# Seventy chunks of U products ahead of the V products in the first layer, where sixty-four were

## The chip, the cores and the metric

The kernel runs on one core of a Trainium2 chip. The metric is the time of one execution on the device in microseconds (us): the median of three runs of the kernel before is 2871.74 us (2870.99 to 2872.57). TensorE is called PE here, its weight loads PEld, VectorE DVE, ScalarE ACT, GpSimd POOL and SyncE SP.

## The reference

Two layers work on 256 latent tokens and 256 context tokens of width 1024. The first layer mixes tokens with a gated MLP, the second with a bidirectional state-space scan (S5); after each mixer comes a PEER block, in which every token picks experts out of 16384. The PEER block is what the change is about:

```python
def block(hb):
    q = (hb @ w_q).reshape(PEER_BLOCK, PEER_HEADS, 2, PEER_DHALF)
    s = jnp.einsum("nhkd,hkmd->nhkm", q, sub_keys)
    s_half, i_half = lax.top_k(s, PEER_TOPK)
    cand = s_half[:, :, 0, :, None] + s_half[:, :, 1, None, :]
    top_s, top_c = lax.top_k(cand.reshape(...), PEER_TOPK)
    ...
    ids = k1 * PEER_KEYS + k2
    g = jax.nn.softmax(top_s, axis=-1)
    ue = jnp.take(u_tab, ids, axis=0)
    ve = jnp.take(v_tab, ids, axis=0)
    act = jax.nn.gelu(jnp.einsum("nd,nhkd->nhk", hb, ue))
    return jnp.einsum("nhk,nhkd->nd", g * act, ve)
```

Each token so uses 8 heads x 16 experts = 128 rows of the table U (16384 x 1024) and the same 128 rows of the table V.

## The kernel before

**Two ways through the PEER block.** In the first layer (layer 0 in the code) 384 of the 512 tokens go through all 16384 experts densely, with a gate matrix that is zero where a token did not pick an expert. The tables are cut into 128 chunks of 128 experts. The other 128 tokens, the last of the context, go by gathers: POOL issues an indirect DMA (line 600) that brings one 4 KB row of U or V for each of 128 tokens, 512 KB in all; for a row of U DVE makes dot products (`gscr`, line 610), for a row of V it adds to the sum `acc` (line 623). There are 128 gathers of U and 128 of V, in turns of 16, into four buffers (`ROWS`); an issue waits until DVE has used the buffer four rows earlier.

**U product of a chunk** (`front`): the loads `ur` (512 KB), its split into a high part `uh` on ACT and a rest `ul` on DVE, 24 matmuls over 384 columns (lines 304 to 306; three for each of eight blocks, since the product of split numbers needs three), and a gelu on ACT (`act`, line 717). **V product of a chunk** (`back`): the load `vr` (512 KB), its split into `vh` (ACT) and `vl` (DVE), the gated activations `w` and their split `wh`, `wl`, and 18 matmuls over 512 columns (lines 753 to 755) that add into six PSUM banks. It also brings 192 KB of gates (`Gr`), and 192 KB of activations (`actr`) where the U product was made long before and its `act` written to memory (`act_d`).

**Order.** `dense` runs three stretches. First come the U products of the first `ahead` = `AHEAD0` chunks; between them stands the routing (top 16, one-hot products) and the building of the gates of three blocks of 128 tokens on DVE, PE and ACT (lines 641 to 679). All but the last two of these U products come before the end of the gate work. Of the activations all but the last `keep` = 8 are written to memory. Then the V products alone, until chunk `ahead - keep`; beside them run the phase tables of the second layer (lines 905 to 932), a few modulation rows (`adasv`, line 218) and the first 18 steps (36 rows) of the gathers. From there on one U and one V product alternate, and after the last U product eight V products follow. The gathers' other 110 steps are spread over this stretch.

```python
for k1 in range(ahead - TF[i]):
    front(k1, k1 < ahead - keep)
    during(k1)
between()
with tc.issue_after(ends["gates"]):
    for k1 in range(ahead - TF[i], ahead):
        front(k1)
...
for k1 in range(KEYS):
    if ahead <= k1 + keep < KEYS:
        front(k1 + keep)
        done += 1
    back(k1)
    done += 1
    pump(done / total)
```

In that last loop PE's order is the written one. On the other engines, and on PE ahead of it, a scheduler sets the order when the kernel is built, from due times of its own; each engine then runs its list strictly in turn. At the end `add_back` transposes the four sums on PE (line 586) and DVE adds them to the token state `XT` (line 328). The second layer starts with the norm of all 512 tokens and so needs the gathered sum `acc` too; its loads `kT` and `wqT` stand on SP behind the last use of the gathers' buffers, its first weights `s5w`, split into `s5wh` (ACT) and `s5wl` (half on DVE, half on POOL), behind the transposes of the dense sums.

Of the kernel before, what the change touches and what calls it, by code (L numbers as in the profile page):

```python
# [42 lines left out]
NST = 64  # L43
L = 8
NDENSE = 384
AHEAD0 = 64
TAIL0 = 0
WB = 2
KEEP0 = 8
# [57 lines left out]
def tile_hybrid(ctx: ExitStack, tc: tile.TileContext, I, out, stop=None):  # L107
# [15 lines left out]
    def use_banks(*b):  # L123
        banks[0] = list(b)
# [6 lines left out]
    def pool(name, bufs=1, side=None):  # L131
        return tc.tile_pool(name=name, bufs=bufs, side=side, reuse_waits="tile")
# [72 lines left out]
    def ada_rows(pa, blocks, cB=None, e=nc.vector):  # L205

        k = "g" if e is nc.gpsimd else "v"
        if cB is None:
            cB = ada_silu(pa)
        for i, f in blocks:  # L210
            w = pa.tile([P, D], F32, name=f"adat{k}")
            r0 = f * P - (0 if i else 3 * D)
            load(w, I[f"ada_t{i}"][r0:r0 + P, :])
            nt = parts_of(i, f)
            for t in range(nt):
                if e is nc.vector:
                    scr = pa.tile([P, D], F16, name=f"adas{k}", bufs=1)
                    e.scalar_tensor_tensor(scr, w, 1.0, cB[:, t], op0=OP.mult, op1=OP.mult,  # L218
                                           accum_out=mod[:, i, f, t:t + 1])
                else:  # L220
                    scr = pa.tile([P, D], F32, name="adap", bufs=1) if t == 0 else w
                    e.tensor_tensor(scr, w, cB[:, t], op=OP.mult)
                    nc.scalar.activation(scr, scr, AF.Copy, accum_out=mod[:, i, f, t:t + 1])
            if f % 8 == 7:
                m = mod[:, i, f - 7:f + 1, 0:nt]
                nc.vector.tensor_tensor(m, m, ab[:, i, f - 7:f + 1].unsqueeze(2).to_broadcast([P, 8, nt]), op=OP.add)
                scale_cols(i, f - 7, 8)
            yield
# [1009 lines left out]
    def spread(*items):  # L1238

        state = [[g, n, a, b, 0] for g, n, a, b in items]  # L1240

        def pump(t):
            for s in state:
                g, n, a, b, _ = s
                while s[4] < n * min((t - a) / (b - a), 1.0):
                    s[4] += next(g, None) or 1
        return pump

    def layer0():
# [53 lines left out]
        with pool("hx") as ph, pool("hold", side="right") as pk, ExitStack() as hold:  # L1303
# [57 lines left out]
            with pool("de0", 2) as pd, ExitStack() as rs:  # L1361
# [4 lines left out]
                def during(k):  # L1366
                    first((k + 1) / (AHEAD0 - TAIL0 - TF[0]))

                def between():
# [5 lines left out]
                    ada = ada_rows(pa, LATE[NS:NQ], cB)  # L1375
                    cut = (AHEAD0 - KEEP0) / (2 * KEYS - AHEAD0)
                    rest.append(spread((gathers, MID0, 0.0, cut), (gathers, 128 - early - MID0, cut, GEND), (phases, 29, *PW),
# [4 lines left out]
                def back_work(t):  # L1382
                    with tc.issue_after(ends["w"]) if PB_ <= t < PC_ else ExitStack():
                        rest[0](t)

                use_banks(2, 3, 4, 5, 6, 7)
                dense(pd, lambda: rs.enter_context(pool("db0", 2, side="right")), 0, n, hh, hl, AHEAD0, KEEP0, (0, 1), (2, 3, 4, 5, 6, 7),
                      during, between, back_work)
# [173 lines left out]
```

## Time and profile before

| | |
|---|---|
| median of three runs | 2871.74 us |
| the profiled execution: its own time | 2873.85 us |
| its span, first to last instruction | 2872.1 us |
| PE busy | 2640.3 us, 92% |
| DVE busy | 2233.4 us, 78% |
| mean granted clock of TensorE | 0.955 |

The dense part of the first layer lies from 492 us (gelu of its first U product) to 1735 us (last gathered row added) of the span. Rows of "windows" give for a stretch the busy time of each engine with the number of instructions, the granted clock and the DMA engines' mean busy share. A row of a timeline is one instruction, or several of one kind merged: start, duration, engine, line, operation, what it writes and reads, and in brackets how long the engine sat idle before it and what ended that.

### The profile page before, as it was taken

What the parts mean: (1) busy time and instruction counts of PE and PEld (TensorE: products, weight loads), DVE (VectorE), ACT (ScalarE), POOL (GpSimd) and SP (SyncE); (2) the same over time, 40 slices, a digit from 0 to 9 for tenths busy, and PEclk for the clock granted to TensorE, in tenths of its full rate; (3) what the DMA queues carried; (4) which work ended last, traced back from release to release, by engine and by line L of the source; (5) the groups of instructions that cost most, each with busy time, mean ns of one, the idle gap of its engine ahead of it and who ended that gap; (6) DMA issues with size and microseconds to landing.
All of it is one profiled execution on the core that took longest, in us unless ns stands there. A gap on an engine that the chain in (4) does not pass through costs nothing.

```text
span 2872.1 us, 43897 instructions
## 1 busy us (share of the span) xinstructions
PE 2640.3 (92%) x16231; PEld 2360.2 (82%) x16231; DVE 2233.4 (78%) x3964; ACT 1233.6 (43%) x1900; POOL 562.6 (20%) x429
## 2 busy tenths in 40 slices
PE   6799979998968899999999987898899999999998
PEld 2499878998956677999999976898888988899997
DVE  7795889999978677888888876474899867755555
ACT  5453242364653233333333324334456654444443
POOL 2032121000100212544444441235300000000000
PEclk8899989999979999999999998999899999999999
DMA  8569843564758888999999988996468989866652
GB/s 274 169 214 352 276 157 130 177 214 169 251 212 288 305 295 275 355 339 338 339 338 338 333 300 297 329 328 176 142 208 276 316 287 296 264 205 214 212 200 103
DMA packets 414560, 738.76 MB, mean 257 GB/s; under 512 B 41605, under 2 KB 272261, under 8 KB 409225
## 3 DMA queue, kind: packets, MB, share of 16 engines
q1 hardware_dynamic: 310240, 507.84, 53.2%
q0 software_dynamic: 36864, 134.23, 13.1%
q10 hardware_dynamic: 67240, 93.88, 9.3%
q8 instruction: 127, 2.08, 0.3%
q14 instruction: 89, 0.72, 0.1%
HBM read 633.07 MB, written 102.77 MB: 256 GB/s over the span
## 4 chain that ended last, share of the span: by engine, by line
PE 51%; DMA 8%; DVE 7%; issue 3%; ACT 1%; POOL 1%; SPq 0%; ACTq 0%; DVEq 0%; POOLq 0%
PE bk L754 8%; PE bk L306 8%; PE bk L755 8%; PE bk L304 8%; PE bk L753 8%; PE bk L305 8%; DMA vr<-peer_v 2%; PE bk L553 1%; DMA row<-peer_v,ids 1%; DVE vl L298 1%; DMA ph_d<-ph 1%; DVE ul L298 1%; DMA actr<-act_d 1%; DMA wp<-wpo 1%; PE bk L1151 1%
## 5 line engine op out<-in xcount | busy, mean ns | idle before, releaser
L304 PE MATMUL bk<-hxh,uh 128*128 128x384 f32 (+1 forms) x2048 | 644.4, 315 | 23.1 <-ACT act L717 14.4
L306 PE MATMUL bk<-hxh,ul 128*128 128x384 f32 (+1 forms) x2048 | 641.1, 314 | 14.0 <-DVE ul L298 14.0
L305 PE MATMUL bk<-hxl,uh 128*128 128x384 f32 (+1 forms) x2048 | 638.8, 312 | 0.0
L754 PE MATMUL bk<-vl,wh 128*128 128x512 f32 x1280 | 510.4, 399 | 26.0 <-DVE vl L298 24.5
L753 PE MATMUL bk<-vh,wh 128*128 128x512 f32 x1280 | 506.8, 396 | 24.1 <-ACT vh L296 16.9
L755 PE MATMUL bk<-vh,wl 128*128 128x512 f32 x1280 | 506.7, 396 | 0.6 <-DVE wl L298 0.6
L296 ACT ACTIVATE uh<-ur 128x1024 fp32r<-128x1024 f32 x256 | 271.5, 1061 | 512.4 <-PE bk L305 446.2
L304 PEld LDWEIGHTS bk<-hxh,uh 128*128 128x128 f32 x2048 | 394.2, 192 | 33.3 <-ACT act L717 19.1
L298 DVE TENSOR_TENSOR ul<-ur,uh 128x1024 fp32r<-128x1024 f32 x256 | 313.0, 1223 | 136.0 <-ACT uh L296 134.6
L306 PEld LDWEIGHTS bk<-hxh,ul 128*128 128x128 f32 x2048 | 393.5, 192 | 18.3 <-DVE ul L298 18.3
L305 PEld LDWEIGHTS bk<-hxl,uh 128*128 128x128 f32 x2048 | 394.2, 193 | 4.6
L298 DVE TENSOR_TENSOR vl<-vr,vh 128x1024 fp32r<-128x1024 f32 x256 | 313.1, 1223 | 50.0 <-ACT vh L296 40.8
L296 ACT ACTIVATE wh<-w 128x384 fp32r<-128x384 f32 (+1 forms) x256 | 120.6, 471 | 494.2 <-PE bk L754 465.1
L754 PEld LDWEIGHTS bk<-vl,wh 128*128 128x128 f32 x1280 | 244.6, 191 | 83.3 <-DVE vl L298 34.1
L753 PEld LDWEIGHTS bk<-vh,wh 128*128 128x128 f32 x1280 | 244.9, 191 | 77.5 <-ACT vh L296 20.8
L296 ACT ACTIVATE vh<-vr 128x1024 fp32r<-128x1024 f32 x256 | 268.0, 1048 | 82.9 <-DMA vr<-peer_v 69.2
L755 PEld LDWEIGHTS bk<-vh,wl 128*128 128x128 f32 x1280 | 244.5, 191 | 52.7 <-DVE wl L298 1.6
L298 DVE TENSOR_TENSOR wl<-w,wh 128x384 fp32r<-128x384 f32 (+1 forms) x256 | 125.6, 491 | 165.3 <-ACT wh L296 158.1
L600 POOL DMA_INDIRECT row<-peer_u,ids x128 | 169.3, 1323 | 274.7 <-DVE gscr L610 166.7
L600 POOL DMA_INDIRECT row<-peer_v,ids x128 | 163.8, 1280 | 239.0 <-DVE acc L623 162.2
L218 DVE SCALAR_TENSOR_TENSOR adasv<-adatv,cB 128x1024 f16<-128x1024 f32 x112 | 148.8, 1329 | 55.8 <-DMA adatv<-ada_t 54.7
L623 DVE SCALAR_TENSOR_TENSOR acc<-row,wts,acc 128x1024 f32<-128x1024 f32 x127 | 162.6, 1281 | 13.3 <-DMA row<-peer_v,ids 12.7
(324 smaller groups left out, 4453.0 us busy)
## 6 DMA issues: line engine op xcount, KB each, us to landing
ur<-peer_ut SPq DMA_DIRECT2D x256, 512.0 KB
vr<-peer_v SPq DMA_DIRECT2D x256, 512.0 KB
gd<-Gs ACTq DMA_DIRECT2D x40, 1024.0 KB
adatv<-ada_t SPq DMA_DIRECT2D x72, 512.0 KB
wqT<-peer_w_q SPq DMA_DIRECT2D x64, 512.0 KB
Gr<-gd SPq DMA_DIRECT2D x120, 192.0 KB
wp<-wpo ACTq DMA_DIRECT2D x32, 512.0 KB
wpi<-wp SPq DMA_DIRECT2D x16, 1024.0 KB
```

The costliest lines, as they stand in the source:

```text
L218: e.scalar_tensor_tensor(scr, w, 1.0, cB[:, t], op0=OP.mult, op1=OP.mult, accum_out=mod[:, i, f, t:t + 1])
L296: nc.scalar.activation(hi, src, AF.Copy)
L298: return e.tensor_tensor(lo, src, hi.bitcast(F32), op=OP.subtract)
L304: nc.tensor.matmul(o, ah, bh, start=(i == 0), stop=False)
L305: nc.tensor.matmul(o, ah, bl, start=False, stop=False)
L306: last = nc.tensor.matmul(o, al, bh, start=False, stop=(i == n - 1))
L553: nc.tensor.matmul(pm[:, d * P:(d + 1) * P], ws[b][:, ds], kT[:, b], start=(b == 0), stop=(b == 1))
L600: tc.keep_in_program_order(nc.gpsimd.indirect_dma_start(out=r[:], out_offset=None, in_=I[f"peer_{table}{i}"], in_offset=bass.IndirectOffse ...
L623: nc.vector.scalar_tensor_tensor(acc, r, w, acc, op0=OP.mult, op1=OP.add)
L753: nc.tensor.matmul(o, wh[:, js], vh[:, qs], start=first, stop=False)
L754: nc.tensor.matmul(o, wh[:, js], vl[:, qs], start=False, stop=False)
L755: nc.tensor.matmul(o, wl[:, js], vh[:, qs], start=False, stop=last)
```

## The change

One number: `AHEAD0` goes from 64 to 70.

```diff
-AHEAD0 = 64
+AHEAD0 = 70
```

Seventy U products then stand in the first stretch, 68 of them between the gate work; 62 of their activations are written to memory and read back, where 56 were. 62 V products stand alone before the alternation begins, where 56 did, and 58 pairs follow, where 64 did. The count of products, of gates and of gathered rows stays. The steps of the gathers are counted out over the new numbers: 36 rows over the V products alone, the others up to 97% of the alternation.

On DVE, at the end of the first stretch, where the gates of the third block are built (`eq` and `o` are one-hot matrices, `ul` is the split for a U product). Before:

```order
L675 TENSOR_TENSOR eq<-iot,kt_7736 128x2048 x3
L647 CAST gt_7738<-gs 128x128
L648 TENSOR_TENSOR gt_7738<-gs,gt_7738 128x128
L679 TENSOR_TENSOR o_7745<-eq,gt_7738 128x1024
L679 TENSOR_TENSOR o_7784<-eq,gt_7738 128x1024
L679 TENSOR_TENSOR o_7810<-eq,gt_7738 128x1024
```

At the same place of DVE's list now:

```order
L298 TENSOR_TENSOR ul<-ur,uh 128x1024 x2
L675 TENSOR_TENSOR eq<-iot,kt_7906 128x2048 x3
L647 CAST gt_7908<-gs 128x128
L298 TENSOR_TENSOR ul<-ur,uh 128x1024
L648 TENSOR_TENSOR gt_7908<-gs,gt_7908 128x128
L679 TENSOR_TENSOR o_7949<-eq,gt_7908 128x1024
```

Before, no split of a U product stood in the third block until its end; now five stand among its first rows (three of them here, two a few rows on), and the gates of the second block have 21 U products beside them where 18 were.

On DVE, from the split of the last V product on (`acc` is one gathered row, `XT` a sum added to the token state). Before:

```order
L298 TENSOR_TENSOR vl<-vr,vh 128x1024
L623 SCALAR_TENSOR_TENSOR acc<-row,wts,acc 128x1024 x5
L328 SCALAR_TENSOR_TENSOR XT<-bk_15830,mod,XT 128x128 x4
L328 SCALAR_TENSOR_TENSOR XT<-bk_15839,mod,XT 128x128 x4
L623 SCALAR_TENSOR_TENSOR acc<-row,wts,acc 128x1024
L328 SCALAR_TENSOR_TENSOR XT<-bk_15851,mod,XT 128x128 x4
L328 SCALAR_TENSOR_TENSOR XT<-bk_15860,mod,XT 128x128 x4
L623 SCALAR_TENSOR_TENSOR acc<-row,wts,acc 128x1024
L328 SCALAR_TENSOR_TENSOR XT<-bk_15872,mod,XT 128x128 x4
L328 SCALAR_TENSOR_TENSOR XT<-bk_15881,mod,XT 128x128 x4
L328 SCALAR_TENSOR_TENSOR XT<-bk_15891,mod,XT 128x128 x4
L328 SCALAR_TENSOR_TENSOR XT<-bk_15900,mod,XT 128x128 x4
```

The list of now reads the same for the split, the five rows and two groups of `XT` with a row between; from the seventh row behind the split on it is:

```order
L623 SCALAR_TENSOR_TENSOR acc<-row,wts,acc 128x1024
L328 SCALAR_TENSOR_TENSOR XT<-bk_15890,mod,XT 128x128 x4
L328 SCALAR_TENSOR_TENSOR XT<-bk_15899,mod,XT 128x128 x2
L623 SCALAR_TENSOR_TENSOR acc<-row,wts,acc 128x1024
L328 SCALAR_TENSOR_TENSOR XT<-bk_15899,mod,XT 128x128 x2
L623 SCALAR_TENSOR_TENSOR acc<-row,wts,acc 128x1024
L298 TENSOR_TENSOR s5wl<-s5w,s5wh 128x512
L623 SCALAR_TENSOR_TENSOR acc<-row,wts,acc 128x1024
L298 TENSOR_TENSOR s5wl<-s5w,s5wh 128x512
L623 SCALAR_TENSOR_TENSOR acc<-row,wts,acc 128x1024 x13
L328 SCALAR_TENSOR_TENSOR XT<-bk_15909,mod,XT 128x128 x4
L328 SCALAR_TENSOR_TENSOR XT<-bk_15918,mod,XT 128x128 x4
```

Behind the last V product seven gathered rows stood before (5 + 1 + 1); now 23 do (5 + 1 + 1 + 1 + 1 + 1 + 13), and two splits of the second layer's weights stand among them.

On POOL, which issues the gathers, the end of the list was before:

```order
L600 DMA row<-peer_u,ids 128x1024 x16
L600 DMA row<-peer_v,ids 128x1024 x32
L298 TENSOR_TENSOR s5wl<-s5w,s5wh 128x512 x8
L1086 MEMSET dec_16644 128x512
L1086 MEMSET dec_16645 128x512
```

Now it is:

```order
L600 DMA row<-peer_v,ids 128x1024 x21
L298 TENSOR_TENSOR s5wl<-s5w,s5wh 128x512
L600 DMA row<-peer_v,ids 128x1024
L298 TENSOR_TENSOR s5wl<-s5w,s5wh 128x512
L600 DMA row<-peer_v,ids 128x1024 x10
L298 TENSOR_TENSOR s5wl<-s5w,s5wh 128x512 x6
```

Two splits that stood behind all gathers now stand ahead of eleven and of ten of their issues.

## Rows read from the trace of the kernel before

**Rows 1.** The page's 40 equal slices (71.8 us each), busy share in tenths.

```profile
PE   6799979998968899999999987898899999999998
DVE  7795889999978677888888876474899867755555
DMA  8569843564758888999999988996468989866652
```

**Rows 2.** Windows by stretch: busy us (x instructions), granted clock, DMA share, GB/s.

```profile
core 0: us, PE busy (x) PEld busy (x) DVE busy (x) ACT busy (x) POOL busy (x), PEclk, DMA share, GB/s
700.00:800.00 100.00, 92.20 (x684) 89.06 (x682) 98.34 (x218) 58.95 (x74) 13.53 (x17) 0.97 0.61 216
800.00:855.00 55.00, 35.15 (x307) 30.28 (x307) 44.36 (x57) 35.23 (x40) 0.00 (x0) 0.75 0.52 197
855.00:1000.00 145.00, 118.83 (x449) 91.78 (x450) 111.89 (x216) 39.51 (x53) 21.63 (x27) 0.91 0.88 298
1000.00:1148.00 148.00, 136.83 (x586) 109.55 (x585) 103.72 (x148) 49.02 (x66) 27.72 (x22) 0.99 0.85 286
1148.00:1655.00 507.00, 507.00 (x2565) 461.59 (x2564) 429.02 (x535) 179.38 (x251) 248.88 (x186) 1.00 0.95 339
1655.00:1720.00 65.00, 54.44 (x228) 44.46 (x226) 45.46 (x47) 15.24 (x21) 26.95 (x23) 0.89 0.90 318
1720.00:1736.00 16.00, 9.40 (x41) 6.92 (x41) 14.08 (x29) 4.28 (x8) 4.04 (x4) 0.77 0.29 99
```

**Rows 3.** DVE groups from 492 to 855 us: busy, mean ns, idle before.

```profile
L298 DVE TENSOR_TENSOR ul<-ur,uh 128x1024 fp32r<-128x1024 f32 x64 | 78.4, 1228 | 12.3 <-ACT uh L296 11.8 <-issue 0.4
L679 DVE TENSOR_TENSOR o<-eq,gt 128x1024 f16<-128x1024 f16 x96 | 60.9, 686 | 0.0
```

**Rows 4.** ACT's timeline: gelu of two U products of the alternation, 56 pairs apart.

```profile
1165.34 0.47 ACT L717 ACTIVATE act<-bk 128x384 f32<-128x384 f32 x1
...
1630.51 0.47 ACT L717 ACTIVATE act<-bk 128x384 f32<-128x384 f32 x1
```

**Rows 5.** Windows of line 755 alone (six matmuls to a V product).

```profile
1000.00:1148.00 148.00, 73.35 (x187) 35.39 (x187) 0.99 0.85 286
```

**Rows 6.** Waits from 855 to 1148 us: us in total, times, longest.

```profile
ACT vh L296 <- DMA vr<-peer_v: 49.2, 25, 6.2
PEld bk L754 <- DVE vl L298: 27.9, 21, 4.5
```

**Rows 7.** Windows of the gathers' issues on POOL (line 600) alone.

```profile
1000.00:1148.00 148.00, 27.72 (x22) 0.99 0.85 286
1165.00:1630.00 465.00, 224.06 (x170) 1.00 0.96 342
```

**Rows 8.** DVE's timeline from the split of the last V product on.

```profile
1719.01 1.23 DVE L298 TENSOR_TENSOR vl<-vr,vh 128x1024 fp32r<-128x1024 f32 x1 [4.79 <-ACT vh L296]
1720.15 5.24 DVE L623 SCALAR_TENSOR_TENSOR acc<-row,wts,acc 128x1024 f32<-128x1024 f32 x4
1727.21 1.28 DVE L623 SCALAR_TENSOR_TENSOR acc<-row,wts,acc 128x1024 f32<-128x1024 f32 x1 [1.82 <-DMA row<-peer_v,ids]
...
1733.75 1.27 DVE L623 SCALAR_TENSOR_TENSOR acc<-row,wts,acc 128x1024 f32<-128x1024 f32 x1
```

**Rows 9.** POOL's timeline there: the last three issues and the next split.

```profile
1721.70 1.86 POOL L600 DMA_INDIRECT row<-peer_v,ids  x1 [6.28 <-DVE acc L623]
1723.87 1.02 POOL L600 DMA_INDIRECT row<-peer_v,ids  x1 [0.30 <-issue]
1725.19 1.01 POOL L600 DMA_INDIRECT row<-peer_v,ids  x1 [0.30 <-issue]
1735.86 1.27 POOL L298 TENSOR_TENSOR s5wl<-s5w,s5wh 128x512 fp32r<-128x512 f32 x1 [9.65 <-ACT s5wh L296]
```

**Rows 10.** The chain that ended last, there: start, us, what.

```profile
1721.49 0.21 issue
1721.70 5.42 DMA row<-peer_v,ids
...
1736.11 2.16 PE bk L586 x8
...
1739.34 5.28 DMA wqT<-peer_w_q
```

## The prediction

> **What bounds the kernel now.** I read the page's slices first, then the windows by stretch, then the rows of single lines at the seams.
>
> The slices show PE at 8 or 9 for most of the span, with two hollows that touch this change: slice 12 (6, from 790 to 862 us) and slices 24 and 25 (8 and 7, from 1651 to 1795 us) [rows 1]. The windows cut the dense part of the first layer into four stretches with four different limits [rows 2].
>
> - *First stretch, 492 to 855 us: U products beside routing and gates.* From 700 to 800 us DVE is busy for 98.3 of 100 us and PE for 92.2; from 800 to 855 us, where the third block's gates are built after almost all U products, DVE is busy for 44.4 and PE for only 35.2 of 55 us. DVE leads, PE follows closely.
> - *V products alone, 855 to 1148 us.* PE is busy for 118.8 of 145 us and then for 136.8 of 148; the DMA engines for 88% and 85%. The waits name the load of `vr` ahead of ACT's split (49.2 us in 25 waits), and PE's weight loads wait for `vl` behind it [rows 6].
> - *Alternation, 1148 to 1655 us.* PE is busy all 507 us at clock 1.00. 56 pairs take 1630.51 - 1165.34 = 465.2 us [rows 4], 8.31 us a pair. A U product streams 24 x 384 = 9216 columns and a V product 18 x 512 = 9216, so each costs half, 4.15 us.
> - *End, 1655 to 1736 us.* Eight V products take 65 us, then the last gathered rows run alone: from 1720.15 us, after the last split for a V product, to 1735.03 us DVE adds seven rows [rows 8]. PE has nothing to do until the transposes at 1736.11 us, and the loads of the second layer go out behind them [rows 10].
>
> **The change part by part.** Six U products go from the alternation into the first stretch, six V products from the alternation into the stretch of V products alone, and 16 gathered rows from the cover of PE's work to the bare end.
>
> *Six pairs leave the alternation.* 6 x 8.31 = 49.8 us less. PE is busy without a gap there, so this is taken off the path in full, as long as the remaining 58 pairs keep their pace. They do if the gathers beside them stay as dense: 170 issues fall on 56 pairs [rows 7], 3.0 a pair, and DVE's list has 3.1 a pair now as before (159 rows between the splits of the 69th and 121st V product in both). DMA stays at its 95%.
>
> *Six U products enter the first stretch.* Each brings 4.15 us of PE and 1.23 us of DVE for `ul` [rows 3]. Three of them come into the second block's gates (21 beside it where 18 were): PE 92.2 + 12.5 = 104.7, DVE 98.3 + 3.7 = 102.0, in what was 100 us; I take +6. Three come to the head of the third block: PE 35.2 + 12.5 = 47.7 and DVE 44.4 + 3.7 = 48.1, both under 55 us, but the two engines wait for each other there, so I take DVE's 3.7, +4. Together +10. The ends: 0, if the idle time of both engines swallows them; 6 x 4.15 = 24.9, if PE's work is paid in full. The sum is nearer to DVE's 7.4 than to PE's 24.9, since DVE is the busier engine. Six more writes of `act` (192 KB each) meet a DMA share of 0.52 to 0.61 and cost nothing; if they did not find room, 1.2 MB at 216 GB/s would be 5 us.
>
> *Six V products enter the stretch without U products.* The second half of that stretch holds 187 / 6 = 31.2 of them [rows 5] in 148 us, 4.75 us each, of which PE is busy for 136.8 / 31.2 = 4.39 us [rows 2]. The gathers there grow by almost nothing (DVE has used 38 rows by the 57th V product before, 36 by the 61st now), so the loads that hold PE up get no denser; I take PE's busy time, 6 x 4.39 = +26. The ends: 6 x 4.75 = 28.5; and 19.2, if only transport counts (6 x 896 KB at 286 GB/s).
>
> *Sixteen rows more stand behind the last V product*, 23 where seven were, since the scheduler kept three rows to a pair and there are six pairs fewer. They run in a ring of four buffers: the issue at 1721.70 us lands 5.42 us later [rows 10], DVE adds for 1.28 us [rows 8] and POOL issues again 0.21 us after that [rows 10]: 6.9 us for four rows, 1.73 us a row, 16 x 1.73 = 28 us. On top, two splits of `s5w` now stand in the middle on DVE and POOL. The second `s5w` load goes out only behind the transposes of the dense sums; a 512 KB load lands in 5.28 us [rows 10] and POOL's half of the split takes 1.27 us [rows 9], and with ACT's half some 7.7 us pass in which POOL issues no row. Three rows in flight cover 3 x 1.28 of it: +4. Together +32. Nothing of it is covered: PE's next work is the transpose of that very sum, then the norm. `kT` and `wqT` still wait for the last row. The ends: POOL's own issue spacing, 1725.19 - 1723.87 = 1.32 us [rows 9], 16 x 1.32 = 21; and the mean of the seven last rows, 14.9 / 7 = 2.13 us [rows 8], 34 us, with the 7.7 us whole: 42.
>
> The Trainium skill speaks on that row: its page "DMA: Bandwidth & Descriptors", section "Anatomy of one DMA — SWDGE (gpsimd) path", fits a transfer issued by GpSimd with 2.0 us plus its bytes over 436e3 per us, for a row of 512 KB 3.2 us, an estimate from that page. By it the ring would take 3.2 + 1.28 + 0.21 = 4.7 us for four rows, POOL's 1.32 us would set the pace, and the sum below would be 11 us lower. The trace's 5.42 us, of which POOL's own instruction holds 1.86, speaks against it, and the trace decides.
>
> *The sum.* +10 + 26 - 49.8 + 32 = +18 us. The profiled execution took 2873.85 us (span 2872.1), so it would take 2892; the median of the runs shown is 2.1 us below it, and the forecast for a median is 2890. The terms' ends give 0 + 19 - 50 + 21 = -10 and 25 + 28.5 - 50 + 42 = +46.
>
> **The rivals.**
>
> *The bare rows and the V products run at transport price.* Tail 21, V products 19: 10 + 19 - 50 + 21 = 0, 2872. For it: the DMA share is only 0.29 from 1720 to 1736 us [rows 2], so the rows meet little traffic. Against it: that window has a landing of 5.42 us in it all the same, and PE alone needs 24.9 us for six V products, more than transport.
>
> *The U products are paid in full in the first stretch, and the tail at its upper end.* 25 + 26 - 50 + 42 = +43, 2915. For it: from 700 to 800 us PE and DVE are both over 92% busy, and the two engines take turns. Against it: from 800 to 855 us PE idles for 20 us, and three of the six fall there.
>
> *The last eight V products run free* (the other side). They took 65 us and cost PE 8 x 4.15 = 33; 32 us are stalls, in which DVE waits for ACT's `vh` (4.79 us before the last one, [rows 8]) and that for its load. If these loads find the DMA queues emptier, 18 - 32 = -14, 2858; it ends below no change as soon as more than 18 of the 32 us go. For it: 17 rows fewer have been gathered by then. Against it: the rows among the last eight V products are as many (15 where 14 stood in DVE's list), so the loads compete with as much.
>
> That the change does not do what it says is ruled out by the lists: U and V products stand 70, 62 and 58 as meant.
>
> **How the numbers follow.** The forecast (+8 to +28, 2880 to 2900) has 0.62, the full price (+28 to +46) 0.15, transport price (-6 to +8) 0.16, the free V products 0.07. A measurement can tell 0.2%, 5.7 us, from no change: faster 0.07, same 0.16, slower 0.77. The range leaves out the free V products, the lower part of the transport case and the uppermost part of the full price: 2873 to 2910.
>
> **What would show it.** Right: the gelu of the last U product of the first stretch about 10 us later than the seam at 855 us; then about 26 us more from the first to the last lone V product; pairs still 8.31 us apart with PE at 1.00 clock; and between the last `vl` and the last `acc` some 47 us where 14.9 were, with POOL's issues about 1.7 us apart and one gap around the splits of `s5w`. Wrong: pairs slower than 8.31 us, which would say that DMA at 95% is the bound; a first stretch longer by 20 us or more; or a tail under 30 us, which would say that a row's landing of 5.42 us was that of a loaded queue. If the time falls, the last eight V products are the place to look.

## The result, and the profile after

The changed kernel took 2890.96 us in the median of five runs (2882.45 to 2891.95), the kernel before 2871.74 us in runs beside it: a ratio of 1.0051, 95% interval 1.0031 to 1.0070 (the medians differ by 19.2 us, the means of the five runs by 2888.1 - 2872.6 = 15.5 us). The forecast was slower, 2890 us; that it lies 1 us from the median is closer than these runs can tell, since a second series of the same two kernels (e1_again below) has the medians 16.0 us apart.

The profiled execution of the changed kernel took 2882.45 us, with a span of 2880.7 us. Its page's slices (as in [rows 1], now 72.0 us each):

```profile
PE   6799979999988789999999965998889999999998
DVE  7795879999987766888888876474899967755555
DMA  8569843556658988899999888997367989866652
```

On PE slice 12 has filled from 6 to 8, and slices 24 and 25, which hold the bare end, have sunk from 8 and 7 to 6 and 5. Windows of the changed kernel by stretch (columns as in [rows 2]):

```profile
core 0: us, PE busy (x) PEld busy (x) DVE busy (x) ACT busy (x) POOL busy (x), PEclk, DMA share, GB/s
700.00:800.00 100.00, 96.43 (x701) 90.98 (x700) 99.20 (x219) 56.95 (x71) 16.42 (x17) 0.98 0.64 230
800.00:868.80 68.80, 56.68 (x435) 52.03 (x434) 53.37 (x66) 45.13 (x54) 0.00 (x0) 0.85 0.57 206
868.80:1184.00 315.20, 276.58 (x1145) 220.57 (x1146) 230.22 (x383) 99.38 (x134) 46.50 (x49) 0.95 0.87 290
1184.00:1655.00 471.00, 471.00 (x2383) 428.82 (x2382) 397.68 (x496) 164.86 (x232) 234.59 (x176) 1.00 0.95 339
1656.60:1705.00 48.40, 35.33 (x143) 27.16 (x143) 33.57 (x45) 11.06 (x15) 18.47 (x16) 0.89 0.93 334
1705.00:1723.00 18.00, 9.89 (x45) 7.36 (x43) 16.25 (x34) 4.57 (x8) 7.98 (x8) 0.73 0.65 208
1723.00:1753.60 30.60, 0.00 (x0) 0.00 (x0) 22.51 (x17) 1.15 (x2) 18.42 (x14) 0.50 0.77 255
```

The alternation is still wall to wall PE at clock 1.00. The last row is the price: 30.6 us in which PE does nothing at all, while DVE is busy for 22.5 us and POOL for 18.4 us, with the rows, their issues and two splits of `s5w` on each of the two.

The seams are read from ACT's gelu: the last one of the first stretch, the first and second of the alternation, and those of its 54th and last (58th) U product.

```profile
868.81 0.47 ACT L717 ACTIVATE act<-bk 128x384 f32<-128x384 f32 x1
...
1183.93 0.47 ACT L717 ACTIVATE act<-bk 128x384 f32<-128x384 f32 x1
...
1192.23 0.47 ACT L717 ACTIVATE act<-bk 128x384 f32<-128x384 f32 x1
...
1624.18 0.47 ACT L717 ACTIVATE act<-bk 128x384 f32<-128x384 f32 x1
...
1656.61 0.49 ACT L717 ACTIVATE act<-bk 128x384 f32<-128x384 f32 x1 [2.94 <-PE bk L306]
```

From the second to the 54th are 52 pairs in 1624.18 - 1192.23 = 431.95 us, 8.31 us each, as before.

DVE's timeline from the split of the last V product on (as [rows 8]):

```profile
1703.82 1.23 DVE L298 TENSOR_TENSOR vl<-vr,vh 128x1024 fp32r<-128x1024 f32 x1 [2.54 <-ACT vh L296]
1704.96 5.24 DVE L623 SCALAR_TENSOR_TENSOR acc<-row,wts,acc 128x1024 f32<-128x1024 f32 x4
1711.84 1.28 DVE L623 SCALAR_TENSOR_TENSOR acc<-row,wts,acc 128x1024 f32<-128x1024 f32 x1 [1.64 <-DMA row<-peer_v,ids]
1713.04 2.15 DVE L328 SCALAR_TENSOR_TENSOR XT<-bk,mod,XT 128x128 f32<-128x128 f32 x8
...
1724.63 2.28 DVE L623 SCALAR_TENSOR_TENSOR acc<-row,wts,acc 128x1024 f32<-128x1024 f32 x1
...
1727.44 4.00 DVE L623 SCALAR_TENSOR_TENSOR acc<-row,wts,acc 128x1024 f32<-128x1024 f32 x2
1732.22 1.28 DVE L623 SCALAR_TENSOR_TENSOR acc<-row,wts,acc 128x1024 f32<-128x1024 f32 x1 [0.78 <-DMA row<-peer_v,ids]
1736.02 2.61 DVE L623 SCALAR_TENSOR_TENSOR acc<-row,wts,acc 128x1024 f32<-128x1024 f32 x2 [2.52 <-DMA row<-peer_v,ids]
...
1752.34 1.28 DVE L623 SCALAR_TENSOR_TENSOR acc<-row,wts,acc 128x1024 f32<-128x1024 f32 x1 [0.30 <-DMA row<-peer_v,ids]
1754.84 1.38 DVE L328 SCALAR_TENSOR_TENSOR XT<-bk,mod,XT 128x128 f32<-128x128 f32 x5 [1.21 <-PE bk L586]
```

POOL's timeline beside it (as [rows 9]), from the issue ahead of the first split of `s5w` to the last issue:

```profile
1722.66 0.94 POOL L600 DMA_INDIRECT row<-peer_v,ids  x1 [1.81 <-DVE acc L623]
1723.62 2.21 POOL L298 TENSOR_TENSOR s5wl<-s5w,s5wh 128x512 fp32r<-128x512 f32 x1
1725.98 1.76 POOL L600 DMA_INDIRECT row<-peer_v,ids  x1 [0.15 <-issue]
1727.76 1.27 POOL L298 TENSOR_TENSOR s5wl<-s5w,s5wh 128x512 fp32r<-128x512 f32 x1
1729.19 1.75 POOL L600 DMA_INDIRECT row<-peer_v,ids  x1 [0.16 <-issue]
...
1747.21 0.94 POOL L600 DMA_INDIRECT row<-peer_v,ids  x1 [1.69 <-DVE acc L623]
```

From the end of the last `vl` (1705.0) to that of the last `acc` (1753.6) are 48.6 us, where 14.8 were. Nine spacings from the issue at 1729.19 to that at 1747.21 make 2.00 us a row; around the two splits it is 3.3 and 3.2 us. POOL begins both splits at once, without a wait; its first takes 2.21 us where the second takes 1.27, and DVE's adds beside them take 2.28 us and 4.00 us for two, where an add elsewhere takes 1.28. The list of DMA issues from 1710 to 1752 us gives the median of 17 rows from issue to landing, in us:

```profile
row<-peer_v,ids POOLq DMA_INDIRECT x17, 6.0
```

And the chain that ended last (as [rows 10]) goes through the last row into the transposes and the first load of the second layer:

```profile
1747.21 5.04 DMA row<-peer_v,ids
...
1752.34 1.29 DVE acc L623
...
1753.68 1.98 PE bk L586 x8
...
1756.74 5.55 DMA wqT<-peer_w_q
```

**One table for all traces.** Five marks cut the first layer's dense part: *first* is from the first gelu to the last one of the U products ahead; *lone V* from the end of the first `vl` to the first gelu of the alternation; *pairs* from there to the gelu of the last U product; *last V* to the end of the last `vl`; *end* to the first tile of the second layer (`hT5h`, line 319). Each line is one profiled execution; "traced" is its sum less that of before, "timed" the difference of the medians of many runs, beside runs of the kernel before on the same chip. "Rows behind" are the gathered rows behind the last `vl` in DVE's list.

| kernel | first | lone V | pairs | last V | end | traced | timed | rows behind |
|---|---|---|---|---|---|---|---|---|
| before | 361.7 | 296.3 | 522.5 | 49.0 | 37.6 | | | 7 |
| after | 374.8 | 316.6 | 472.7 | 48.4 | 71.7 | +17.1 | +19.2 | 23 |
| e1_again | 374.1 | 317.5 | 472.7 | 48.4 | 72.2 | +17.8 | +16.0 | 23 |
| e2_mid26 | 375.0 | 336.6 | 472.7 | 51.1 | 40.7 | +9.0 | +4.8 | 7 |
| e3_a67 | 365.2 | 313.4 | 497.6 | 48.7 | 57.7 | +15.5 | +9.1 | 16 |
| e4_mid34 | 373.3 | 359.5 | 470.7 | 42.1 | 38.0 | +16.5 | +5.7 | 0 |
| e5_g1_64 | 361.8 | 294.3 | 522.5 | 35.2 | 34.7 | -18.6 | -18.8 | 0 |
| e6_g1_70 | 374.1 | 329.6 | 472.7 | 35.1 | 37.2 | -18.4 | -22.5 | 0 |
| e7_rows5_70 | 375.5 | 319.8 | 472.7 | 53.4 | 57.1 | +11.4 | +6.6 | 17 |
| e8_rows5_64 | 362.9 | 295.2 | 522.5 | 46.8 | 35.8 | -3.9 | -9.5 | 2 |
| e9_mid10_64 | 361.7 | 277.9 | 522.5 | 51.8 | 71.9 | +18.7 | +12.7 | 22 |
| e10_mid26_64 | 361.7 | 323.3 | 522.5 | 41.2 | 30.9 | +12.5 | +9.6 | 0 |
| e11_rows5_mid14 | 361.9 | 283.2 | 522.5 | 51.1 | 41.0 | -7.4 | -6.3 | 8 |

The stretch *pairs* lies between two gelus and so holds one pair less than the name says (57 steps of 58 pairs after the change). Traced and timed agree within 7 us in all but one line (e4, 11 us apart); the second layer, whose code is the same in all of them, moves by as much from one execution to the next, as the first experiment shows.

### The profile page after: what moved, and what is told of

The parts are those of the page before. It is cut to its first block, busy times and chain, and to the rows that moved or that the text cites. A ratio compares the mean times of both kernels' runs of the same rounds, so it can differ in the third digit from the quotient of the medians.

```text
span 2880.7 us, 43923 instructions
## 1 busy us (share of the span) xinstructions
PE 2628.1 (91%) x16231; PEld 2350.0 (82%) x16231; DVE 2237.2 (78%) x3964; ACT 1233.9 (43%) x1900; POOL 561.7 (19%) x429
## 3 DMA queue, kind: packets, MB, share of 16 engines
q0 software_dynamic: 36864, 134.23, 13.1%
## 5 line engine op out<-in xcount | busy, mean ns | idle before, releaser
L304 PEld LDWEIGHTS bk<-hxh,uh 128*128 128x128 f32 x2048 | 391.9, 191 | 35.2 <-ACT act L717 19.3
L298 DVE TENSOR_TENSOR vl<-vr,vh 128x1024 fp32r<-128x1024 f32 x256 | 313.0, 1223 | 49.7 <-ACT vh L296 41.2
```

The source lines that it names most:

```text
L298: return e.tensor_tensor(lo, src, hi.bitcast(F32), op=OP.subtract)
L304: nc.tensor.matmul(o, ah, bh, start=(i == 0), stop=False)
```

## The experiments

**e1_again: the changed kernel once more.** The profiled execution of the changed kernel lies 8.5 us under the median of its runs; a second trace was to show where such a difference sits. The edit is that of the change.

> The changed kernel once more, nothing edited, for a second trace of it: its runs so far lie in two groups, 2882 to 2883 and 2891 to 2892 us, and the one that was profiled is of the lower group. If the two groups come from the second layer, the stretches up to the last gathered row stay within 2 us of the first trace (last row added 48.6 us after the split of the last V product) and only a stretch behind it moves by some 8 us. If they come from the gathered rows at the bare end, that 48.6 moves by some 8 us.

2891.46 us, ratio 1.0056 (1.0036 to 1.0076). Its trace repeats every stretch of the first layer within 1 us, but spans 2896.1 us where the trace of after spans 2880.7. Of the 15.4 us between them 4.3 lie ahead of the first gelu (494.0 and 498.3 us) and 10.5 behind the first tile of the second layer, in its first matmul stretch and in its dense part. Windows of those two stretches, in the trace of after:

```profile
1776.70:1961.40 184.70, 174.64 (x1340) 160.84 (x1340) 112.03 (x157) 71.72 (x136) 50.53 (x32) 0.98 1.01 328
...
2093.20:2843.20 750.00, 732.00 (x5012) 668.21 (x5011) 547.43 (x856) 401.48 (x575) 0.00 (x0) 1.00 0.73 244
```

and in that of e1_again:

```profile
1781.60:1972.20 190.60, 178.66 (x1340) 164.00 (x1340) 112.14 (x156) 71.72 (x136) 50.67 (x32) 0.96 1.00 319
...
2102.60:2858.60 756.00, 738.97 (x5008) 674.55 (x5007) 547.60 (x856) 401.59 (x573) 0.00 (x0) 0.99 0.74 242
```

Nearly the same number of recorded matmuls takes PE 4.0 and 7.0 us longer, at a granted clock of 0.96 for 0.98 and 0.99 for 1.00. The kernel before had the longer form in its trace (190.1 and 756.0 us). So the profiled execution of after hides some 10 us of its loss in the second layer; the stretches of the first layer have to be compared, not the spans.

**e2_mid26 and e4_mid34: the rows back under cover.** The gathers' steps beside the lone V products (`MID0`, two rows each) are raised, so that seven rows stand behind the last V product again, or none.

```diff
-AHEAD0 = 64
+AHEAD0 = 70
...
-MID0 = 18
+MID0 = 26
```

> AHEAD0 stays 70, MID0 goes from 18 to 26: 16 gathered rows more stand beside the V products that run alone, and seven instead of 23 behind the last V product. Theory (the loss is rows that run bare): from the split of the last V product to the last row 15 us instead of 48.6; the lone V products get longer by less than that, 8 to 20 us; in all 14 to 26 us faster than the changed kernel, 2865 to 2877. Rival (DMA transport is the bound of that stretch, so rows cost the same wherever they stand): the lone V products get longer by 16 x 512 KB at 290 GB/s = 29 us or more, and the time stays within 5 us of the changed kernel.

2880.28 us, ratio 1.0022 (1.0010 to 1.0034). The end goes from 71.7 back to 40.7 us, and the lone V products pay 20.0 us for the 16 rows, 1.25 us each. About 11 us of the loss are gone (2891.46 - 2880.28, the medians of e1 and e2): the sign is the theory's, the size falls short of its 14 us, as the rows cost the upper end of its 8 to 20 us beside the lone V products.

With `MID0 = 34` instead:

> AHEAD0 70, MID0 34: 32 rows more beside the lone V products, none behind the last V product. Theory: the bare end goes to about 0, 48 us less than in the changed kernel; the lone V products pay for 32 rows; if a row costs PE 0.5 to 1.2 us there, 16 to 38 us, so 10 to 32 us faster than the changed kernel. Rival (transport): 32 rows cost 58 us there and the time is 5 to 15 us above the changed kernel.

2881.17 us, ratio 1.0018 (1.0005 to 1.0030). Sixteen more rows moved and nothing gained: the lone V products took another 22.9 us, the last eight V products gave 9.0 us back, the end only 2.7 us: 38.0 us with no row behind it. Against the changed kernel (e1) it is 10.3 us faster, the lower edge of the theory. DVE's timeline there shows what the end is without rows:

```profile
1739.49 1.22 DVE L298 TENSOR_TENSOR vl<-vr,vh 128x1024 fp32r<-128x1024 f32 x1 [2.73 <-ACT vh L296]
1747.13 5.29 DVE L328 SCALAR_TENSOR_TENSOR XT<-bk,mod,XT 128x128 f32<-128x128 f32 x20 [6.42 <-PE bk L586]
```

The last matmuls of the V product, the transposes and the adds to `XT` run behind the last split in any case. The seven rows of the kernel before lay beside them.

**e3_a67: half the change.**

```diff
-AHEAD0 = 64
+AHEAD0 = 67
```

> AHEAD0 67, half the change. 16 rows stand behind the last V product in DVE's list (7 before, 23 at 70). Theory: every term halves: first stretch +6, lone V products +10, alternation -25, bare rows +18, in all +5 to +10 us against the kernel before. Rival (the loss is a step, from the two splits of the second layer's weights that stand among the rows at 70, or from one more stall in the gates): bare rows under +10 us, and the time within 3 us of the kernel before, or slower already by as much as at 70.

2884.5 us, ratio 1.0033 (1.0019 to 1.0047), about half the loss. The three pairs give 24.9 us, the end takes 20.1 for nine more rows. From 67 to 70 chunks the end grows by another 14.0 us for seven rows, 2.0 us each. The two splits of `s5w` stand among the rows in DVE's timeline of e3 already, so these 14.0 us hold no step from them, and the rival falls. Two terms don't halve. The first stretch grows by 3.5 us for the first three U products and by 9.6 for the second three; the lone V products by 17.1 us for the first three and by 3.2 for the second three, where +10 was expected. Why they are so uneven is not shown.

**e5_g1_64 and e6_g1_70: almost no gathers.** Only one head of eight is gathered (32 rows instead of 256), with 64 and with 70 chunks ahead.

```diff
-gathers = gather_units(pg, 0, hn, gk[3][0], ids, HEADS, lambda acc: add_back(0, acc, n, P))
+gathers = gather_units(pg, 0, hn, gk[3][0], ids, 1, lambda acc: add_back(0, acc, n, P))
```

> The kernel before (AHEAD0 64) with only one head of the gathers: 32 gathered rows instead of 256, so the last 128 context tokens get one eighth of their PEER sum, and nothing is gathered in the alternation or behind it. It is the partner of the next run. Theory: the alternation keeps 8.31 us a pair (PE is its bound); the stretch from the split of the last V product to the first modulated tile of the second layer stays at about 38 us, since seven rows are hidden there. Rival (DMA sets the alternation at 95% share): pairs get shorter than 8.2 us.

> The changed kernel (AHEAD0 70) with the same 32 gathered rows. Theory: without rows behind the last V product the change is a gain, first stretch +13, lone V products +20, alternation -50: 15 to 20 us less than its partner with AHEAD0 64. Rival (the loss is in the first two stretches or in contention of the loads, the rows only look late): it stays as slow as, or slower than, its partner by 5 us or more.

2857.76 and 2854.13 us (ratios to before 0.9937 and 0.9919). Without rows at the end the loss is gone: 70 is 3.6 us faster than 64 in the medians of four runs each, which overlap (2851.4 to 2860.5 and 2855.2 to 2861.8 us), and the two traces are equal within 0.2 us. The theory's gain of 15 us or more did not appear, nor did the rival's loss of 5: the pairs give the full 49.8 us, the first stretch takes 12.3, but the lone V products take 35 us where 20 were expected. The test is disturbed there: with few gathers in the list the scheduler drew 14 modulation rows into that stretch, where the changed kernel and e5 have 8. From 1150 to 1200 us of e6 DVE waits for the loads of these rows:

```profile
DVE adasv L218 <- DMA adatv<-ada_t: 6.3, 2, 4.3
```

That accounts for a part of the 15 us; the rest is not located. So these two runs show that the loss goes with the rows, not what the U products' move is worth. What they settle is the pairs. A window of the alternation of e6:

```profile
1200.00:1640.00 440.00, 440.00 (x2226) 400.82 (x2226) 195.94 (x236) 154.23 (x213) 0.00 (x0) 1.00 0.50 161
```

With DMA at half its time instead of 95% and DVE at 45% instead of 84%, the stretch of 58 pairs takes the same 472.7 us. PE alone sets that pace; neither DMA nor DVE was a hidden bound. And without rows the last eight V products take 35 us instead of 49: the 14 us of the rival in which they run free are there to be had, but not by this change.

**e7_rows5_70: five buffers for the rows.**

```diff
-AHEAD0 = 64
+AHEAD0 = 70
...
-ROWS = 4
+ROWS = 5
```

> The changed kernel with five buffers for gathered rows instead of four; DVE's list then has 17 rows behind the last V product where 23 stand with four. Theory (a ring of buffers sets the pace of the bare rows): the pace falls from 2.1 us a row to 1.4 to 1.7, the bare end from 48.6 to 24 to 30 us, the whole 15 to 25 us faster than the changed kernel, about 2866 to 2876. Rival (POOL, DVE or transport sets the pace): 2.1 us a row as before, 17 x 2.1 = 36 us, 10 to 13 us faster.

2883.18 us, ratio 1.0023 (1.0009 to 1.0036). The end falls by 14.6 us to 57.1, with 17 rows behind where 23 were, so six rows of the fall are a matter of place; 5.0 us of it come back in the last V products (53.4 us), which hold 19 rows where 15 stood. By the medians it is 9 to 13 us faster than the changed kernel (+6.6 against +16.0 and +19.2), as the rival had it and short of the theory's 15 to 25. POOL's timeline behind the splits:

```profile
1734.41 1.26 POOL L298 TENSOR_TENSOR s5wl<-s5w,s5wh 128x512 fp32r<-128x512 f32 x1 [5.67 <-ACT s5wh L296]
...
1738.69 1.22 POOL L600 DMA_INDIRECT row<-peer_v,ids  x1 [0.15 <-issue]
1740.22 0.94 POOL L600 DMA_INDIRECT row<-peer_v,ids  x1 [0.30 <-issue]
1741.46 0.95 POOL L600 DMA_INDIRECT row<-peer_v,ids  x1 [0.31 <-issue]
1742.72 1.01 POOL L600 DMA_INDIRECT row<-peer_v,ids  x1 [0.30 <-issue]
```

Behind the stall the issues come every 1.2 to 1.5 us and none waits for DVE, where the changed kernel's waited up to 2.0 us for `acc`. But they fill a ring that ran empty during the stall, so they show POOL's own spacing, not a pace that five buffers sustain. In the stall itself POOL stands idle for 5.67 us for `s5wh`, with the last five issues queued behind its split; in the changed kernel it reached that split later and began it at once (1723.62 us). Over all, 57.1 us is 14.6 us below the changed kernel; with six rows fewer behind, 6 x 2.00 = 12 us of that is the rows' number. The other 2.6 us, and whatever the stall of 5.67 us hides, are all that a faster ring can have given.

**e8_rows5_64 and e11_rows5_mid14: five buffers without the change.** The first has `ROWS = 5` alone, the second also `MID0 = 14`.

> The kernel before with five buffers for gathered rows; two rows stand behind the last V product where seven did. Theory: the end is a floor of about 38 us from the split of the last V product to the first modulated tile of the second layer, under which seven rows were hidden already, so nothing is gained there; the time stays within 6 us of the kernel before. Rival (the rows were still on the path before): 10 us or more faster than the kernel before.

> The kernel before with five buffers for the gathered rows where four were (ROWS 5) and 14 steps beside the lone V products where eighteen were (MID0 14); 64 U products ahead as before. DVE's list has 8 rows behind the last V product, two with five buffers alone. Theory (up to some seven rows behind the last V product are hidden, a row beside the lone V products costs 1.25 us): lone V products 295 to 285 (-10), last vl to first tile of the second layer 36 to 38, so about 8 us under five buffers alone (2867 there) and 18 under the kernel before: about 2858. Rival (a row costs the same wherever it stands, the DMA engines being what it takes): no difference from five buffers alone, about 2867.

2867.12 us, ratio 0.9970 (0.9956 to 0.9984), and 2869.94 us, ratio 0.9985 (0.9973 to 0.9997). Five buffers alone make the fastest kernel that does all the work, by 0.3%; the trace shows 3.9 us of it, in pieces of 1 to 2 us over the lone V products, the last V products and the end, and the rest is not located. The 9.5 us between the medians lie outside the theory's 6 and just under the rival's 10, so this run decides for neither. Moving eight rows out of the lone V stretch on top takes 12.0 us there and gives 4.3 and 5.2 us back in the last V products and at the end; timed it brought nothing. There the rival's number was right; its reason, that a row costs the same wherever it stands, does not hold in the alternation, where e5 and e6 show rows at no cost.

**e9_mid10_64: the rows alone.** No U product is moved; 16 rows fewer stand beside the lone V products, and 22 behind the last one.

```diff
-MID0 = 18
+MID0 = 10
```

> The kernel before with one number changed: ten steps of the gathers beside the lone V products where eighteen were (MID0 10). No U product is moved; 64 stand ahead as before. DVE's list has 22 gathered rows behind the last V product, where seven were in the kernel before and 23 in the changed kernel. Theory (only the rows beyond the first seven cost, some 2 us each at the bare end; and a row beside the lone V products costs 1.25 us there): last vl to first tile of the second layer 38 to about 70 us (+32), lone V products 296 to about 276 (16 rows less, -20), pairs and first stretch as before; sum +12, about 2887 beside a kernel before of 2875. Rival (the bare end of the changed kernel is due to its U products, whose written activations or loads disturb it, and rows alone run free there): end as before, 38, lone V -20, sum -20, about 2855.

2888.96 us, ratio 1.0041 (1.0028 to 1.0054). This is the test that settles the matter. DVE's timeline at its end:

```profile
1704.55 1.23 DVE L298 TENSOR_TENSOR vl<-vr,vh 128x1024 fp32r<-128x1024 f32 x1 [10.65 <-ACT vh L296]
...
1735.16 1.28 DVE L623 SCALAR_TENSOR_TENSOR acc<-row,wts,acc 128x1024 f32<-128x1024 f32 x1 [0.64 <-DMA row<-peer_v,ids]
1738.73 2.60 DVE L623 SCALAR_TENSOR_TENSOR acc<-row,wts,acc 128x1024 f32<-128x1024 f32 x2 [2.28 <-DMA row<-peer_v,ids]
...
1748.37 3.93 DVE L623 SCALAR_TENSOR_TENSOR acc<-row,wts,acc 128x1024 f32<-128x1024 f32 x3 [1.49 <-DMA row<-peer_v,ids]
```

It has nearly the same waits, the same gap behind the splits of `s5w` and the same end, 71.9 us, as the changed kernel's 71.7, and all three parts of the theory came true (end +34.3 us, lone V products -18.4, the median +12.7). The end grew by 34.3 us for 15 rows with no U product moved: the loss at the end belongs to the rows alone.

**e10_mid26_64: the other way.** With `MID0 = 26` and 64 chunks ahead, no row stands behind the last V product.

> The kernel before with 26 steps of the gathers beside the lone V products where eighteen were (MID0 26), so that DVE's list has no gathered row behind the last V product. 64 U products stand ahead as before. Theory (the seven rows at the end of the kernel before lie under the chain of last matmuls, transposes and norm): last vl to first tile of the second layer stays about 38 us, lone V products +20 (16 rows at 1.25 us), eight rows fewer are in the alternation but PE keeps its 8.31 us a pair; the last eight V products lose some of their rows, up to -10; sum +10 to +20, about 2890. Rival (the seven rows are on the path for their 14.8 us): end about 23, sum -5 to +5, about 2875.

2885.85 us, ratio 1.0028 (1.0017 to 1.0039). The lone V products take 27.0 us more (1.7 us a row, where e2 has 1.25 and e9 1.15), the last V products 7.8 less, the end 6.7 less (30.9 us), where the theory had it unchanged and the rival at 23. So of the 14.8 us of the seven rows in the kernel before, 0 (e4) to 7 (e10) were on the path, the rest lay under the end that is there anyway.

## Why the prediction was right, point by point

- **Six pairs leave the alternation, -49.8.** As forecast: 522.5 - 472.7 = 49.8 us, in all traces with 70 chunks ahead but e4, where it is 51.8. The reason given, PE without a gap, is shown by e5 and e6.
- **Six U products in the first stretch, +10.** Measured +13.1 (12.3 to 13.8 in the other kernels with 70 ahead and no more than 26 steps beside the lone V products, 11.6 in e4). The choice of the lower half was right; the size came out a third too small. The prediction priced the two engines apart and added a little for turns. Between the stretch's marks DVE's busy time grows by 355.0 - 345.8 = 9.2 us and its idle time by 3.9 (15.9 to 19.8), while PE's idle time falls from 34.1 to 22.4 us. So DVE sets the price, as the prediction said; it had 7.4 us for DVE's work and 2.6 for the turns. In e3 three products cost 1.2 us each, and the next three 3.2.
- **Six V products alone, +26.** Measured +20.3, 3.4 us each: near the lower end of 19.2. The mis-sized term is the 4.39 us of PE for a product. PE's busy time was the right thing to price: between the marks of the stretch it grows from 257.0 to 277.2 us, while PE's idle time stays (39.3 and 39.4). But the 136.8 us behind the 4.39 also hold 24 matmuls of the alternation's first U product, which PE starts at 1144 us; without its 4.2 us they make 4.25 a product. In the alternation PE's timeline has 4.12 us for a V product and 4.19 for a U product, so six should cost 24.7; the products that stood there before got some 4 us shorter. What shortened them stays open: the rows beside them are as many (40 issues in both traces), and e3 shows that the price of a product there is uneven.
- **Sixteen rows behind the last V product, +32.** Measured +33.8 to the last `acc` and +34.1 to the second layer's first tile. The sum was right, its two parts less so. POOL does wait for `acc` and DVE for rows, as a ring does, but it turned slower than 6.9 us for four rows: nine spacings of 2.00 us make 8.0. A landing took 6.0 us in the median, where the prediction had 5.42 from one issue. That is 0.6 of the 1.1 us; for the rest POOL's issues of up to 1.86 us and the start behind the splits are candidates that no run separates. So it is 2.00 us a row, not 1.73 (2.01 in e1, 1.89 in e9): 16 x 2.00 = 32. The splits then add about (3.3 - 2.0) + (3.2 - 2.0) = 2.5 us, not 4, and not in the way foreseen: there is no gap of 7.7 us for a load. ACT waits 4.70 us for the second `s5w`, but POOL is issuing a row meanwhile and begins its split at once; what the splits cost is their own time on POOL and the longer issues and adds beside them. The Trainium skill's fit for a transfer that GpSimd issues ("DMA: Bandwidth & Descriptors", "Anatomy of one DMA — SWDGE (gpsimd) path"), 3.2 us for such a row as an estimate, does not hold here: the last row landed in 5.04 us, and the quickest of the 256 gathers of this trace in 4.2. (The pace alone, 16 x (1.73 - 1.32), makes 7 us; the prediction's 11 also drop the 4 us of the splits.)
- **The sum, +18.** Traced +17.1. The errors of the terms, +3, -6 and +2, nearly cancel; that the sum came closer than its terms is luck.
- **What it left unsaid.** It priced the 16 further rows in full, rightly, but it did not see that the first seven were mostly covered. It let them "run alone", with nothing for PE to do until 1736.11 us, though [rows 2] has PE busy for 9.40 of the 16 us there: PE ends the last V product's matmuls at 1724.5 us and transposes the dense sums. By e4 and e10, taking them away gains 0 to 7 us of their 14.8.

**The rivals.** *Transport price* needed a tail of 21 us: it was 33.8; only its V products (19) came close to 20.3. *The U products in full* needed 25: it was 13.1. *The last eight V products free* needed them to fall by more than 18 us: they went from 49.0 to 48.4, with as many rows among them as before; e5 shows that 14 us go when the rows go. It could hardly have come true: its 65 us were misread. The window from 1655 to 1720 us holds 48 matmuls of two U products and ten V products; eight take 49.0 us, which leaves 49.0 - 33 = 16 us of stalls, not 32.

What is left open: the worth of the U products' move by itself. e2, with seven rows behind as before, is 4.8 us slower than before; e6 against e5, with hardly any rows, 3.6 us faster in overlapping runs and equal in the traces, but with other work drawn into the stretch. So it lies between a small loss and a small gain, and depends on where the 16 rows go: 34 us at the bare end, 18 to 27 us beside the lone V products (e9, e2, e10), nothing inside the pairs.

## What to carry to other kernels

Work that is pulled out of a stretch bounded by one engine shortens that stretch by its full price, but it also takes away the cover of a side stream that was metered by that stretch. Count the items of the side stream per unit of cover, multiply by the units removed, and look where the rest of them lands; here six pairs at some three rows each made 16 rows of 2 us, which ate two thirds of the 49.8 us. And before pricing the items at an end, find out how long that end is without them: the first few may be free.

## What was not expected of the hardware

- Code that is the same took two lengths in the second layer: 184.7 or 190.6 us and 750.0 or 756.0 us in two executions of one kernel, the longer at a granted clock lower by 0.01 to 0.02. Of one trace against another, spans may mislead by 10 us.
- The stretch of 58 pairs of products took 472.7 us whether the DMA engines were busy for 95% or for 50% of the time, with loads of 512 KB running beside them.
- Behind a stall of 5.7 us and the splits that followed it, the last four issues of gathers by POOL went out 1.2 to 1.5 us apart (e7); in a ring of four buffers that was kept full they went 2.00 us apart (after).
- POOL's first split of `s5w` took 2.20 or 2.21 us, where the second took 1.27, and DVE's add of a row beside the first took 2.28 or 2.29 us, where 1.28 is usual, in each of the four traces in which the two meet (after, e1, e3, e9).
